# Gate and up of a decoder layer as seven half-block products instead of eight

## The chip, the cores and the metric

The kernel runs on one core of a Trainium2 chip. The time is the device time of one execution in microseconds (us); the median of several executions is compared. A profile is taken of one execution and shows each engine's instructions: TensorE (PE, with its weight loads as PEld), VectorE (DVE), ScalarE (ACT), GpSimd (POOL) and SyncE (SP), which issues most of the DMA transfers.

## The reference

One decoder layer on 512 tokens of width 1024, all in float32. An input projection feeds two groups of mixers, a gated linear recurrence and an attention with three branches; their outputs go through an output projection and are added to x. Then comes the part that is changed:

```
h   = rms_norm(x, ffn_norm_w)
out = x + (silu(h @ w_gate) * (h @ w_up)) @ w_down      # 1024 -> 2816 -> 1024
```

## The kernel before

A float32 value enters TensorE as two parts, a high one (rounded to float32r) and a low one (the remainder). A product of two such values is three matmuls: high by high, high by low, low by high (`mm3`, L98 to L101; each matmul is L96). The parts are made on the chip: ScalarE casts the high one, VectorE subtracts it from the value (`weights`, L130 to L153). Where `weights` is told to use GpSimd (12 pieces of the input projection) VectorE is left out: ScalarE writes the negated value, rounded to float32r, into the low tile (L149), and GpSimd issues a DMA that adds the raw value onto it (L150), which leaves the low part. A weight piece is 512 KB; it is loaded into one of three buffers "raw" by SP (L112), and becomes a pair of tiles "whi" and "wlo" with four buffers each.

The order of the instructions is not that of the code alone. A planner simulates the program with costs of its own and lays each engine's instructions into one fixed queue: of those that it holds ready it takes the one that comes first in the code. So matmuls of the feed-forward part may stand between those of the attention. Each engine then runs its queue in order, and SP its transfers.

The attention goes through the token tiles 3, 2, 1, 0 of 128 tokens. When a tile's attention is done, `out_proj` (L864) multiplies its rows with the output weights (12 matmuls of 512 columns for each half of the width, both halves in bank 0) and adds them to the residual `x_sb` (L871), which stays in the on-chip memory. `norm2` (L873) normalises the tile (squares L878, the root on GpSimd L201, the product L884), transposes it in two blocks of 4 x 128 columns (h2p) and splits each into high and low (L890, L891) in the array `ar`. `ar[:, 1]` holds tokens 256 to 511, `ar[:, 0]` tokens 0 to 255.

Gate and up are made in groups of 256 columns of the hidden width, two units of 128 columns each. `load_group` (L938) loads and splits the group's four pieces. `gate_up` (L946) makes, for each unit, 8 steps over the width times 3 matmuls for gate (bank fg) and as many for up (fu), then silu and the product (L956 to L958), and splits the result into high and low (L959, L107). The first two groups (`SPLIT`, L963 to L967) are made in token halves: tokens 256 to 511 first, while tiles 1 and 0 are still under way, then tokens 0 to 255. The other nine groups take all 512 tokens in one matmul. The down projection (fd, L973 to L1003) then runs over the 22 units twice, for each half of the output width, adds the residual and stores.

Of the kernel before, what the change touches and what calls it, by code (L numbers as in the profile page):

```python
# [20 lines left out]
P = 128  # L21
T = 512
# [27 lines left out]
def hybrid_layer(ctx, tc, x, pos, pack, w_in, gate_a, gate_x, qnw, knw, ck1, ck2, cv1, cv2, w_out, fnw, w_gate, w_up, w_down, out):  # L50
# [5 lines left out]
    wst = ctx.enter_context(tc.tile_pool(name="wst", bufs=4))  # L56
# [11 lines left out]
    SLOTS = {"qk": 16, "yr": 8, "rt": 8, "y": 4, "tr": 6}  # L68
# [13 lines left out]

    def small(shape, s, dt=F32, bufs=None):
        return sml.tile(shape, dt, tag=s, name=nm(s), **({} if bufs is None else {"bufs": bufs}))
# [10 lines left out]
    def mm(o, l, r, start, stop):  # L95
        PE.matmul(o, lhsT=l, rhs=r, start=start, stop=stop)  # L96

    def mm3(o, l, r, start, stop):  # L98
        mm(o, l[0], r[0], start, False)
        mm(o, l[0], r[1], False, False)  # L100
        mm(o, l[1], r[0], False, stop)  # L101
# [15 lines left out]
    def weights_in(src, tag):  # L117

        raw = wst.tile([P, 4, 256], F32, tag="raw", bufs=3, name=nm("raw"))
        load(raw, src)  # L120
        out_ = []
        for u in range(2):
            hi, lo = (b2(n, F32R, tag=tag) for n in ("wxh", "wxl"))
            rv = raw[:, 2 * u : 2 * u + 2].rearrange("p a b -> p (a b)")
            S.copy(hi, rv)
            lo_of(lo, rv, hi)
            out_ += [(hi[:, a * 256 : (a + 1) * 256], lo[:, a * 256 : (a + 1) * 256]) for a in range(2)]
        return out_

    def weights(src, a, b, lo_eng=None, row=None, halves=False):  # L130


        raw = wst.tile([P, 1024], F32, tag="raw", bufs=3, name=nm("raw"))
        rv = raw[:, : a * b].rearrange("p (a b) -> p a b", a=a)
        load(rv, src)
        hi = wst.tile([P, 1024], F32R, tag="whi", name=nm("whi"))
        lo = wst.tile([P, 1024], F32R, tag="wlo", name=nm("wlo"))
        n = a * b
        if row is not None:
# [13 lines left out]
        return [tuple(t[:, : a * b].rearrange("p (a b) -> p a b", a=a)[:, i] for t in (hi, lo)) for i in range(a)]  # L153


    x_sb = per.tile([P, NT, D], F32, name="x_sb")
# [5 lines left out]
    def load_x(t):  # L162
        load(x_sb[:, t], x[t * P : (t + 1) * P])
# [57 lines left out]
    def x_half(hf):  # L221
        for k in range(0, KC, 2):
            pt = rot("xT", (4, 5, 6, 7))
            for c in range(2):
                for t in range(2):
                    tp(pt[:, (2 * c + t) * P : (2 * c + t + 1) * P], x_sb[:, 2 * hf + t, (k + c) * P : (k + c + 1) * P])
# [6 lines left out]
    def x_stats():  # L233
        for t in range(NT):
            jk = b2("jk", tag="qk")
            jk2 = b2("jk", tag="qk")
            ss2 = small([P, 2], "ss2")
            after(S.activation(jk, x_sb[:, t, :512], AF.Square, accum_out=ss2[:, 0:1]), pins["x"])
            after(S.activation(jk2, x_sb[:, t, 512:], AF.Square, accum_out=ss2[:, 1:2]), pins["x"])
# [7 lines left out]
    def proj_cm(c0, banks):  # L247
# [3 lines left out]
        def step(w, k, a0, a1):  # L251
            for m in range(4):
                l = tuple(p[:, m * P : (m + 1) * P] for p in w)
                mm3(wide(acc[m][:, a0:a1], a1 - a0), l, hT(k, a0, a1), k == 0 and a0 == 0, k == KC - 1)
# [21 lines left out]
    for t in range(NT):  # L276
        dg = b2("dg", tag="qk")[:, :P]
# [81 lines left out]
    gwr = wst.tile([P, 8, P], F32, tag="raw", bufs=3, name="gwr")  # L359
# [5 lines left out]
    gwh = [b2("gwh", F32R, tag="qk") for _ in range(2)]  # L365
    gwl = [b2("gwl", F32R, tag="qk") for _ in range(2)]
# [14 lines left out]
    for m in range(4):  # L381
# [6 lines left out]
        h, l = b2("xch", F32R, tag="qk"), b2("xcl", F32R, tag="qk")  # L388
# [61 lines left out]
    va = per.tile([P, NT, 2, 2, HD + 1], F32, tag="va", name="va")  # L450
# [5 lines left out]
    zs = []  # L456
    for m in range(4):
        z = b2("z", tag="qk")
# [4 lines left out]
    for m in range(4):  # L463
        tg = []
        for j in range(2):
            pg = rot("pg", (4, 5, 6, 7))
            mm3(pg, (gwh[j][:, m * P : (m + 1) * P], gwl[j][:, m * P : (m + 1) * P]), (xch[m], xcl[m]), True, True)
            tt = b2("tg", tag="yr")
# [565 lines left out]
```

## Time and profile before

| | |
|---|---|
| median of 3 runs | 677.62 us (676.41 to 678.36) |
| the profiled execution | 674.98 us |
| its span, first to last instruction | 673.3 us |
| PE busy / share of the span | 653.8 us / 97% |
| PEld | 541.8 us / 80% |
| DVE | 340.9 us / 51% |
| ACT | 253.2 us / 38% |
| POOL | 40.7 us / 6% |
| mean granted TensorE clock | 0.995 of full speed |

An instruction is named by its line, its engine and what it writes and reads by the program's names. Times of the trace count from the first instruction. Matmuls overlap one another in the pipeline, so their pace is read from the chain of waits (many in a row) and not from the length of one. A DMA's time to landing counts from its issue.

### The profile page before, as it was taken

The numbers are of one execution on the slowest core, as the hardware profiler recorded it, in microseconds if no ns is written. First come the engines' busy times: TensorE is split into PE (matmuls) and PEld (weight loads), VectorE is DVE, ScalarE is ACT, GpSimd is POOL, SyncE is SP. The second block draws the span as 40 slices with busy tenths as digits, with TensorE's granted clock in tenths as the row PEclk, the third lists the DMA queues.
The fourth block names the chain that finished last, engine by engine and source line by source line (L and its number), as shares of the span: only waits on it lengthen the run. The fifth ranks groups of instructions, "written<-read, shape, count | busy, mean of one in ns | idle before, by whom it ended". The sixth has DMA issues, their size and how long they took to land.

```text
span 673.3 us, 8843 instructions
## 1 busy us (share of the span) xinstructions
PE 653.8 (97%) x3486; PEld 541.8 (80%) x3486; DVE 340.9 (51%) x738; ACT 253.2 (38%) x421; POOL 40.7 (6%) x70
## 2 busy tenths in 40 slices
PE   7999989899999999999899999999999999999998
PEld 6878778667788787898798888888888888888886
DVE  6483999865656475956333334434443442223211
ACT  6657958743343343525123223322332232112110
POOL 2111100211001010110000000000000000000000
PEclk9999999899999999999899999999999999999999
DMA  7589743181110010322122244223422343333201
GB/s 264 129 223 203 165 91 115 49 298 65 63 41 24 1 33 0 95 63 91 35 59 68 64 125 125 64 62 125 126 64 63 123 126 93 94 125 126 94 1 62
DMA packets 46914, 64.61 MB, mean 96 GB/s; under 512 B 4052, under 2 KB 32024, under 8 KB 46872
## 3 DMA queue, kind: packets, MB, share of 16 engines
q1 hardware_dynamic: 45064, 57.71, 27.1%
q0 software_dynamic: 1728, 6.29, 5.0%
q8 instruction: 27, 0.44, 0.3%
q14 instruction: 15, 0.12, 0.1%
q10 hardware_dynamic: 80, 0.03, 0.0%
HBM read 55.64 MB, written 2.10 MB: 86 GB/s over the span
## 4 chain that ended last, share of the span: by engine, by line
PE 75%; DVE 8%; issue 7%; DMA 5%; ACT 4%; POOL 1%; POOLq 0%; SPq 0%; DVEq 0%; ACTq 0%
PE fd L96 18%; PE fg L96 18%; PE fu L96 17%; PE po L96 4%; PE por L96 3%; PE sT L96 3%; DMA raw<-in_w_in_dram 3%; PE pw L96 3%; PE s L96 2%; PE ph L96 2%; DMA wlo<-raw 1%; DMA raw<-in_ck_dram 1%; ACT whi L146 1%; PE oc L96 1%; PE ptm L96 1%
## 5 line engine op out<-in xcount | busy, mean ns | idle before, releaser
L152 DVE TENSOR_TENSOR wlo<-raw,whi 128x1024 fp32r<-128x1024 f32 (+2 forms) x73 | 86.4, 1185 | 118.3 <-ACT whi L146 118.3
L146 ACT CAST whi<-raw 128x1024 fp32r<-128x1024 f32 (+2 forms) x85 | 86.8, 1024 | 151.4 <-PE fd L96 75.4
L96 PE MATMUL fu<-ar,whi 128*128 128x512 f32 (+1 forms) x352 | 102.0, 375 | 0.0
L96 PE MATMUL fg<-ar,whi 128*128 128x512 f32 x288 | 90.5, 395 | 0.0
L96 PEld LDWEIGHTS fu<-ar,whi 128*128 128x128 f32 x352 | 63.8, 188 | 13.1
L96 PE MATMUL fd<-wlo,gh 128*128 128x512 f32 (+1 forms) x189 | 69.3, 367 | 0.0
L96 PE MATMUL fd<-whi,gh 128*128 128x512 f32 (+1 forms) x189 | 69.2, 366 | 0.0
L96 PE MATMUL fd<-whi,gl 128*128 128x512 f32 (+1 forms) x189 | 68.9, 366 | 0.0
L96 PE MATMUL fu<-ar,wlo 128*128 128x512 f32 (+1 forms) x176 | 65.8, 375 | 0.1
L96 PEld LDWEIGHTS fg<-ar,whi 128*128 128x128 f32 x288 | 54.1, 188 | 13.0
L96 PE MATMUL fg<-ar,wlo 128*128 128x512 f32 x144 | 57.0, 396 | 0.0
L96 PE MATMUL ptm<-whi,ar 128*128 128x512 f32 (+1 forms) x192 | 53.5, 360 | 2.1 <-DVE qraw L531 1.9
L958 DVE SCALAR_TENSOR_TENSOR ft<-ft,fu 128x512 f32<-128x512 f32 (+1 forms) x26 | 15.7, 605 | 51.2 <-PE fu L96 51.2
L96 PEld LDWEIGHTS po<-va,pe 128*128 128x128 f32 x320 | 39.6, 192 | 2.2 <-ACT pe L815 0.9
L96 PE MATMUL pcm<-ar,whi 128*128 128x512 f32 (+1 forms) x160 | 41.3, 354 | 0.0
L96 PE MATMUL po<-va,pe 128*128 128x65 f32 x320 | 41.0, 272 | 0.3 <-ACT pe L815 0.2
L96 PEld LDWEIGHTS ptm<-whi,ar 128*128 128x128 f32 x192 | 34.3, 188 | 8.1 <-DVE qraw L531 2.3
L96 PEld LDWEIGHTS fd<-whi,gh 128*128 128x128 f32 x189 | 35.6, 189 | 6.1
L96 PEld LDWEIGHTS fd<-wlo,gh 128*128 128x128 f32 x189 | 35.6, 189 | 5.9
L96 PEld LDWEIGHTS fd<-whi,gl 128*128 128x128 f32 x189 | 35.6, 188 | 5.8
L96 PEld LDWEIGHTS fu<-ar,wlo 128*128 128x128 f32 x176 | 33.0, 188 | 6.9 <-DVE wlo L152 0.3
L957 DVE SCALAR_TENSOR_TENSOR ft<-ft,fg 128x512 f32<-128x512 f32 (+1 forms) x26 | 15.6, 604 | 41.3 <-ACT ft L956 41.3
(316 smaller groups left out, 1097.9 us busy)
## 6 DMA issues: line engine op xcount, KB each, us to landing
raw<-in_w_gate_dram SPq DMA_DIRECT2D x22, 512.0 KB, 3.6
raw<-in_w_up_dram SPq DMA_DIRECT2D x22, 512.0 KB, 3.5
raw<-in_w_down_dram SPq DMA_DIRECT2D x22, 512.0 KB, 3.9
raw<-in_w_in_dram SPq DMA_DIRECT2D x16, 512.0 KB, 4.7
wlo<-raw POOLq DMA_DIRECT2D x12, 512.0 KB, 5.9
raw<-in_w_out_dram SPq DMA_DIRECT2D x8, 512.0 KB, 4.5
x_sb<-in_x_dram SPq DMA_DIRECT2D x4, 512.0 KB, 7.8
raw<-in_ck_dram SPq DMA_DIRECT2D x4, 512.0 KB, 4.6
```

The costliest lines, as they stand in the source:

```text
L96: PE.matmul(o, lhsT=l, rhs=r, start=start, stop=stop)
L146: S.copy(hi[:, c], raw[:, c])
L152: (lo_eng or V).tensor_tensor(out=lo[:, c], in0=raw[:, c], in1=f(hi[:, c]), op=ALU.subtract)
L957: V.scalar_tensor_tensor(out=tt, in0=tt, scalar=1.0, in1=pg[:, :nn], op0=ALU.add, op1=ALU.mult)
L958: V.scalar_tensor_tensor(out=tt, in0=tt, scalar=0.5, in1=pu[:, :nn], op0=ALU.mult, op1=ALU.mult)
```

## The change

Gate and up are written as one product of 2 x 2 blocks. A block of the left side is 128 columns of w_gate (A11, A12) or of w_up (A21, A22) by one half of the width; a block of the right side is one half of the width of h by one half of the tokens (B11, B21: tokens 256 to 511; B12, B22: tokens 0 to 255). Instead of eight products of blocks, seven are made, with sums S1 to S4 of blocks of weights and T1 to T4 of blocks of h (Strassen's identity in Winograd's form): A11 B11, A12 B21, S4 B22, A22 T4, S1 T1, S2 T2, S3 T3. Each is 4 pieces x 3 matmuls of 256 columns. Several are added up in one PSUM bank, and ScalarE copies or VectorE adds the running sum out between two of them.

- Sums S are made by VectorE from raw weights (`sums`), and then split; A11 and A12 (`set_gate`) and A22 are split with the DMA that adds (`by_dma`), S1 to S4 by VectorE. `pin` fixes the order of these instructions on each engine.
- Weight loads change from 256 columns by 4 rows to 128 columns by 8 rows per partition (pieces of 512 bytes), still 512 KB each. "whi" and "wlo" become one set of 12 buffers "w"; "raw" keeps 3.
- `norm2` makes two blocks of each of the tiles 3 and 2, and five of each of the tiles 1 and 0.
- Three units (`EARLY`) make A11 B11 and A12 B21 ahead, the rest of all units in one loop, in which the last two products of a unit stand among the first of the next.
- The results of gate and up stay whole until the loop is over; they are split then, into the places of the blocks of h.
- x after the attention goes to a tensor in device memory (`x2`) and is loaded again for the last addition. The scratch for GpSimd's descriptors is 2048.
- In the input projection the matmuls over 512 tokens are made as two of 256.

The core of the diff:

```diff
-    SLOTS = {"qk": 16, "yr": 8, "rt": 8, "y": 4, "tr": 6}
+    SLOTS = {"rt": 8, "y": 4, "tr": 6, "gx": 6}
...
+    def raw_tile(s):
+        return wst.tile([P, 1024], F32, tag="raw", name=nm(s), bufs=3)
+
+    def w_tile(s, dt=F32R):
+        return wst.tile([P, 1024], dt, tag="w", name=nm(s))
...
-                step(ws[a], 2 * kk + a, 0, T)
+                step(ws[a], 2 * kk + a, 0, 256)
+                step(ws[a], 2 * kk + a, 256, T)
...
+        load(x2_dram[i * P : (i + 1) * P], x_sb[i])
...
+        if not late:
+            xn_of[i] = xn
+            for hf in range(2):
+                normed(hf)
+                put(xn[hf], ("11", "21")[hf])
+            return
+        xo = xn_of[i + 2]
+        normed(1)
+        normed(0)
...
+        V.tensor_tensor(out=t3, in0=xn[1], in1=xn[0], op=ALU.subtract)
+        V.tensor_tensor(out=xn[0], in0=xo[0], in1=xn[0], op=ALU.subtract)
+        V.scalar_tensor_tensor(out=t2, in0=xn[1], scalar=-1.0, in1=xn[0], op0=ALU.mult, op1=ALU.subtract)
+        V.scalar_tensor_tensor(out=xo[1], in0=t2, scalar=-1.0, in1=xo[1], op0=ALU.mult, op1=ALU.subtract)
+        for src, n in ((t2, "T2"), (xn[0], "T1"), (t3, "T3"), (xo[1], "T4"), (xn[1], "22")):
+            put(src, n)
...
+    def split(src, hi, lo, by_dma=False):
+        pin("S", S.copy(hi, src))
+        if by_dma:
+            pin("S", S.activation(lo, src, AF.Copy, scale=-1.0))
+            pin("G", G.dma_start(out=lo, in_=src.bitcast(F32R), accum_op=ALU.add))
+        else:
+            pin("V", V.tensor_tensor(out=lo, in0=src, in1=f(hi), op=ALU.subtract))
...
+    def sums(u, r1):
+        r2, sa, sb = raw_tile("r2"), x_tile("sa"), x_tile("sb")
+        w_cols(w_up, u, r2)
+        a11, a12, a21, a22 = r1[:, :512], r1[:, 512:], r2[:, :512], r2[:, 512:]
+        pin("V", V.tensor_tensor(out=sa[:, :512], in0=a21, in1=a22, op=ALU.add))
+        pin("V", V.tensor_tensor(out=sb[:, :512], in0=sa[:, :512], in1=a11, op=ALU.add))
+        pin("V", V.tensor_tensor(out=sb[:, 512:], in0=sb[:, :512], in1=a12, op=ALU.add))
+        pin("V", V.tensor_tensor(out=sa[:, 512:], in0=a11, in1=a21, op=ALU.add))
+        return r2, sa, sb
+
+    def set_sums(u, r2, sa, sb):
+        o = split(sb, w_tile("h"), w_tile("l"))
+        A[u]["S2"], A[u]["S4"] = o[:4], o[4:]
+        o = split(sa, w_tile("h"), w_tile("l"))
+        A[u]["S1"], A[u]["S3"] = o[:4], o[4:]
+        if u < 12:
+            p22 = [b2("p22", F32R, tag="rt") for _ in range(2)]
+        else:
+            p22 = [cst.tile([P, 544], F32R, tag="misc", name=nm("p22"), bufs=3)[:, :512] for _ in range(2)]
+        A[u]["22"] = split(r2[:, 512:], *p22, True)
+
+    def product(o, u, a, b, start):
+        for c in range(4):
+            mm3(o, A[u][a][c], tuple(z[:, c] for z in B[b]), start and c == 0, c == 3, skip_group_check=not start)
...
+    for u in range(NU + 1):
+        if u < NU:
+            g_tile(u)
+            r1 = gate_weights(u)
+            ss = sums(u, r1)
+            if u >= EARLY:
+                set_gate(u, r1)
+            set_sums(u, *ss)
...
+                product(acc_b[u], u, "11", "11", True)
+                S.copy(s1, acc_b[u])
+        if u > 0:
+            product(acc_b[u - 1], u - 1, "22", "T4", False)
+        if EARLY <= u < NU:
+            acc_a[u] = half("fa", 4 + u % 4)
+            product(acc_a[u], u, "12", "21", True)
+            V.tensor_tensor(out=gs[u][:, 256:], in0=acc_a[u], in1=s1, op=ALU.add)
+        if u > 0:
+            product(acc_c[u - 1], u - 1, "S4", "22", False)
+            finish_unit(u - 1)
+        if u < NU:
+            product(acc_b[u], u, "S2", "T2", u < EARLY)
...
+                S.copy(v2, acc_b[u])
+            acc_c[u] = half("fc", 2 * (u % 2) + 1)
+            product(acc_c[u], u, "S1", "T1", True)
+            product(acc_b[u], u, "S3", "T3", False)
...
+                S.copy(v3, acc_b[u])
+            V.tensor_tensor(out=v3, in0=acc_c[u], in1=v3, op=ALU.add)
...
-    nc = _bacc.Bacc("TRN2", target_bir_lowering=False, num_devices=1)
+    nc = _bacc.Bacc("TRN2", target_bir_lowering=False, num_devices=1, dynamic_dma_scratch_size=2048)
```

`finish_unit` adds the bank of S1 T1 and S4 B22 to the copy of A11 B11 and S2 T2 (256 columns), takes the tanh of 512 columns on ScalarE and makes one product of 512 and two of 256 on VectorE.

## Rows read from the trace of the kernel before

**Rows 1.** The page: busy us (share) x instructions; the chain by line.
```profile
PE 653.8 (97%) x3486; PEld 541.8 (80%) x3486; DVE 340.9 (51%) x738; ACT 253.2 (38%) x421; POOL 40.7 (6%) x70
...
PE fd L96 18%; PE fg L96 18%; PE fu L96 17%; PE po L96 4%; PE por L96 3%; PE sT L96 3%; DMA raw<-in_w_in_dram 3%; PE pw L96 3%; PE s L96 2%; PE ph L96 2%; DMA wlo<-raw 1%; DMA raw<-in_ck_dram 1%; ACT whi L146 1%; PE oc L96 1%; PE ptm L96 1%
```

**Rows 2.** The chain in time: start us, us, what, count.
```profile
342.04 2.72 PE fg L96 x24
...
347.48 5.59 PE fg L96 x24
...
543.47 5.60 PE fu L96 x24
549.07 121.08 PE fd L96 x594
```

**Rows 3.** Timeline at the last norm: start us, us, engine, line, count, [idle before].
```profile
303.52 0.69 DVE L107 TENSOR_TENSOR yl<-yTp,yh 128x512 fp32r<-128x512 f32 x1 [1.25 <-ACT yh L854]
...
316.90 0.75 DVE L871 SCALAR_TENSOR_TENSOR x_sb<-pw,ra,x_sb 128x512 f32<-128x512 f32 x1
...
321.45 1.42 DVE L884 SCALAR_TENSOR_TENSOR xn<-x_sb,r,fbc 128x512 f32<-128x512 f32 x2 [0.44 <-POOL r L201]
323.57 0.69 DVE L891 TENSOR_TENSOR ar<-h2p,ar 128x512 fp32r<-128x512 f32 x1 [0.70 <-ACT ar L890]
...
322.26 0.65 PE L104 MATMUL h2p<-ident,xn 128*128 128x128 f32 x4 [3.52 <-DVE xn L884]
```

**Rows 4.** Windows: stretch, length, busy us PE PEld DVE ACT POOL, clock, DMA share.
```profile
306.00:314.00 8.00, 7.87 (x52) 7.00 (x51) 5.12 (x7) 3.70 (x6) 0.00 (x0) 1.00 0.27 79
314.00:322.00 8.00, 4.74 (x33) 4.20 (x31) 5.72 (x11) 4.12 (x7) 0.83 (x1) 1.00 0.55 176
322.00:327.00 5.00, 4.07 (x21) 3.83 (x22) 2.24 (x4) 1.17 (x2) 0.00 (x0) 0.66 0.03 10
```

**Rows 5.** DMA issues: queue, count, KB each, median us to landing.
```profile
raw<-in_w_in_dram SPq DMA_DIRECT2D x16, 512.0 KB, 4.7
```

**Rows 6.** Packets, MB, share of 16 engines: whole span, 350:549, 549:673 us.
```profile
q0 software_dynamic: 1728, 6.29, 5.0%
...
q1 hardware_dynamic: 17627, 18.77, 30.7%
...
q1 hardware_dynamic: 5927, 11.02, 27.4%
```

**Rows 7.** Input projection: chain, GpSimd's timeline, landings of its DMAs.
```profile
26.39 4.78 DMA wlo<-raw
...
31.24 4.55 DMA raw<-in_w_in_dram
...
38.17 1.05 POOL L150 DMA_DIRECT2D wlo<-raw  x1 [8.88 <-ACT wlo L149]
...
L150 POOL DMA_DIRECT2D wlo<-raw x12: 859/862/1074, 26.4 to 85.4; - x12
...
DMA to landing us min/median/max: 4.5/5.9/8.4
```

**Rows 8.** Groups by form from 200 us on: count, busy us, mean ns.
```profile
L146 ACT CAST whi<-raw 128x1024 fp32r<-128x1024 f32 x60 | 63.3, 1055 | 139.5 <-PE fd L96 75.4 <-PE fg L96 27.0 <-PE fu L96 16.8
...
L956 ACT ACTIVATE ft<-fg 128x512 f32<-128x512 f32 x18 | 10.7, 593 | 38.3 <-PE fg L96 38.3
...
L743 ACT COPY pcs<-pc 128x256 f32<-128x256 f32 x2 | 0.7, 353 | 0.0
...
L152 DVE TENSOR_TENSOR wlo<-raw,whi 128x1024 fp32r<-128x1024 f32 x60 | 73.5, 1224 | 114.8 <-ACT whi L146 114.8
...
L107 DVE TENSOR_TENSOR gl<-ft,gh 128x512 fp32r<-128x512 f32 x17 | 11.7, 689 | 6.2 <-ACT gh L959 6.2
...
L958 DVE SCALAR_TENSOR_TENSOR ft<-ft,fu 128x256 f32<-128x256 f32 x8 | 3.3, 419 | 7.1 <-PE fu L96 7.1
```

More of the change, by code (lines that the diff above doesn't have):

```diff
@@ L93, in after, with mm, mm3 @@
         return ins
[L95 to L101, printed above, removed]
+    def mm(o, l, r, start, stop, **kw):
+        PE.matmul(o, lhsT=l, rhs=r, start=start, stop=stop, **kw)
+    def mm3(o, l, r, start, stop, **kw):
+        mm(o, l[0], r[0], start, False, **kw)
+        mm(o, l[0], r[1], False, False, **kw)
+        mm(o, l[1], r[0], False, stop, **kw)
     def tp(o, i, n=P):
@@ L356, in hybrid_layer @@
     V.tensor_scalar(rwn, par[:, R_RW : R_RW + 4], -0.5, None, ALU.mult)
-    gwr = wst.tile([P, 8, P], F32, tag="raw", bufs=3, name="gwr")
+    gwr = raw_tile("gwr").rearrange("p (a b) -> p a b", b=P)
     G.memset(gwr, 0.0)
@@ L447, in dup @@
         return ap.unsqueeze(2).to_broadcast([ap.shape[0], nh, 2, HD])
[L450 removed]
+    va = cst.tile([P, NT, 2, 2, HD + 1], F32, tag="va", name="va")
     G.memset(va[:, :, :, :, HD : HD + 1], 1.0)
@@ new lines, in hybrid_layer, with pin @@
+    chain = {}
+    def pin(k, i):
+        if k in chain:
+            after(i, chain[k])
+        chain[k] = i
+    def split(src, hi, lo, by_dma=False):
[5 more added lines that the diff above has]
+            pin("V", V.tensor_tensor(out=lo, in0=src, in1=f(hi), op=ALU.subtract))
+        return [(hi[:, c * P : (c + 1) * P], lo[:, c * P : (c + 1) * P]) for c in range(src.shape[1] // P)]
@@ new lines, in half, with finish_unit @@
+    def half(s, n):
+        return bank(s, n)[:, :256]
+    acc_a, acc_b, acc_c = {}, {}, {}
+    def finish_unit(u):
+        gate, up, s1, v2, ft = hold[u]
+        if u < EARLY:
+            V.tensor_tensor(out=up[:, 256:], in0=acc_b[u], in1=s1, op=ALU.add)
+        V.tensor_tensor(out=gate[:, :256], in0=acc_c[u], in1=v2, op=ALU.add)
+        S.activation(ft, gate, AF.Tanh, scale=0.5)
+        V.scalar_tensor_tensor(out=gate, in0=ft, scalar=1.0, in1=gate, op0=ALU.add, op1=ALU.mult)
+        if u < EARLY:
+            V.scalar_tensor_tensor(out=gs[u], in0=gate, scalar=-0.5, in1=up, op0=ALU.mult, op1=ALU.mult)
+        else:
+            V.scalar_tensor_tensor(out=gs[u][:, :256], in0=gate[:, :256], scalar=-0.5, in1=up[:, :256], op0=ALU.mult, op1=ALU.mult)
+            V.scalar_tensor_tensor(out=gs[u][:, 256:], in0=gate[:, 256:], scalar=-0.5, in1=acc_b[u], op0=ALU.mult, op1=ALU.mult)
@@ new lines, in hybrid_layer, with g_tile @@
+    gtags = [t for t in ("gx", "y", "rt") for _ in range(SLOTS[t])]
+    def g_tile(u):
+        if u < 4:
+            if u % 2 == 0:
+                gs.extend(b4("g"))
+        else:
+            gs.append(b2("g", tag=gtags.pop(0)))
+    ahead = {}
+    for u in range(EARLY):
+        mk = w_tile if u < 2 else (lambda s: qkp.tile([P, 1024], F32R, tag="qk", name=nm(s), bufs=8))
+        set_gate(u, gate_weights(u), mk)
+        acc_a[u] = half("fa", 4 + u % 4)
+        product(acc_a[u], u, "11", "11", True)
+        xe = cst.tile([P, 544], F32, tag="misc", name=nm("xe"), bufs=3)[:, :512]
+        S.copy(xe[:, :256], acc_a[u])
+        product(acc_a[u], u, "12", "21", False)
+        S.copy(xe[:, 256:], acc_a[u])
+        ahead[u] = xe
@@ L972, in hybrid_layer @@
     NK = DF // P
     TAIL = 4
+    gl_tags = ["tr"] * 2 + ["qk"] * 4 + ["gx"] * 6 + ["y"] * 4 + ["rt"] * 6
+    gh_at = [z.rearrange("p c q -> p (c q)")[:, o : o + 512] for n in ("11", "21", "T2", "T1", "T3", "T4") for z in B[n] for o in (0, 512)]
+    gh = []
+    for k in range(NK):
+        h = gh_at[k]
+        S.copy(h, gs[k])
+        if gl_tags[k] == "qk":
+            if k % 2 == 0:
+                pair = b4("gl", F32R)
+            l = pair[k % 2]
+        else:
+            l = b2("gl", F32R, tag=gl_tags[k])
+        lo_of(l, gs[k], h)
+        gh.append((h, l))
```

211 lines of the change are left out of this document (109 added, 102 removed).

## The prediction

> **What bounds the kernel now.** I read the busy shares of the page first, then the chain of waits in order of time, then windows around the one place where the chain leaves TensorE, then the DMA views. TensorE is busy for 97% of the span, and 35% of the chain is gate and up (fg, fu), 18% the down projection [rows 1]. In order of time [rows 2] each row of 24 matmuls from 347.48 to 549.07 us takes 5.60 us and starts where the last one ends: TensorE never waits there, so only fewer or shorter matmuls can shorten this stage, unless something else becomes late. The same rows price the two shapes: 5.60/24 = 0.2333 us for a matmul of 512 columns, 2.72/24 = 0.1133 us for one of 256. A half-width matmul, with a weight load of its own, costs slightly less than half of a full one. The change lives on that. [...]
>
> **Matmuls.** A unit is 128 columns of gate and of up; there are 22. Before, a unit is 2 x 8 x 3 = 48 full matmuls: 18 units x 48 x 0.2333 = 201.6 us, which is 347.48 to 549.07, and the four split units are 4 x 96 x 0.1133 = 43.5 us. After, a unit is 7 products x 4 pieces x 3 = 84 half matmuls, 9.52 us: 22 x 84 x 0.1133 = 209.4 us. So 35.7 us of TensorE time go. That is the ceiling. The input projection's 144 full matmuls become 288 halves, 33.6 to 32.6 us; that stage waits for transfers [rows 7], so I take nothing, between -1 and +1.
>
> **The start.** Some of the 35.7 us is given back here. Before, 192 half matmuls (21.8 us) on tokens 256 to 511 can run beside the end of the attention; after, only 3 x 24 = 72 (8.2 us). All others need sums over both token halves, so they wait for the norm of the last tile. I rebuild its time from the instructions there [rows 3]: the last attention rows are split at 303.52 + 0.69 = 304.2; 12 output matmuls follow (2.8 us), their addition (0.75), 12 more in the same bank, and the second addition. Before, the second addition ends at 317.65, because fu matmuls stand in TensorE's queue between the two groups; without them I get 304.3 + 2.8 + 1.0 + 2.9 + 0.9 = 311.9. From that addition to the normed rows (316.90 + 0.75 to 321.45) it is 3.8 us, so 315.7; two normalisations and three differences on VectorE, five instructions of about 0.69 (the 512 form of L107) [rows 8], give 319.1; transposing, casting and subtracting T2 takes another 2.2 (322.26 to 324.26 is 2.0 before), so 321.3. I take 322. If the queue keeps its old order it is 317.65 + 3.8 + 3.4 + 2.2 = 327; if planning finds more room, 319. Each of the two late tiles now makes five blocks and four sums: 3 more pairs of cast and subtraction and 4 sums per tile, some 9.4 us more on VectorE. It was busy for 5.12 + 5.72 + 2.24 of the 21 us from 306 to 327 [rows 4], partly with gate and up's own subtractions, which go. So these fit, but the weight sums of units 0 to 2 (4 x 0.6 + 2 x 1.15 = 4.7 us each) compete with them: I take 2 us of delay, from 0 to 8. TensorE will have stood still before it; 5 us at 0.66 is 1.7 us lost, and I take 1.7 again (0 to 4).
>
> **The loop, engine by engine.** ScalarE per unit: four casts or negations of 1024 (1.055 each), two of 512 (0.6), a tanh of 512 (0.6), three copies of 256 out of a bank (0.353 each) [rows 8]: 7.1 us. VectorE: two subtractions of 1024 (1.22), four sums and one product of 512 (0.69), five of 256 (0.42): 8.0 us. Both below 9.52, both above two thirds of it, and each now hands something to TensorE several times per unit: the three copies out of the banks must be done before the next product may add to that bank. The shortest distance is one product, 12 x 0.1133 = 1.36 us, against 0.35 plus at most one cast of 1.05 in front: just enough, so tenths at worst.
>
> **The raw ring.** This is the doubtful part. Each unit loads two raw tiles, as before, into three buffers. But now a raw tile whose low part comes by accumulating DMA is held until that DMA has read it, where VectorE freed it before. The input projection shows such a cycle: the DMA is issued at 26.39, lands after 4.78, the next load into the buffer lands 4.55 after 31.24, and that piece's DMA starts at 38.17: 11.8 us a turn [rows 7]. With the medians (load 4.7 [rows 5], 2.0 for two ScalarE instructions, 0.3 to the issue, landing 5.9 [rows 7]) a gate tile holds its buffer for 12.9 us. An up tile: 4.7, three sums (2.0), four ScalarE instructions (two of 1.0, two of 0.6: 3.2), 0.3, and a landing of half the size, between 2.9 and 5.9, say 4.4: 14.6. Together 27.5 us over three buffers is 9.2 us a unit; with 1 us in each tile's turn for other work of ScalarE and VectorE it is 9.8. At the shortest landings (4.5, and half of it) and without that work it is 8.0, so TensorE bounds; at the longest (8.4, and three quarters of it) 10.6. I take 9.8 us a unit, 0.3 over TensorE's own pace.
>
> **The transfers.** One core's 16 DMA engines carry it all. The accumulating DMA moved 6.29 MB in 5.0% of 16 engines over 673.3 us, 33.7 us [rows 6]: 0.79 MB a unit is 4.2 us. Loads: 18.77 MB in 30.7% of 199 us, 307 GB/s with pieces of 1024 bytes [rows 6]; 1.05 MB is 3.4 us. The new loads have pieces of 512 bytes, which no row shows. By packets, the loads of 350 to 549 us took 61.1 x 16/17627 = 55.5 ns for 1065 bytes, those of 549 to 673 us 34.0 x 16/5927 = 91.7 ns for 1859 bytes; a line through both gives 30 ns for 512 bytes, 3.9 us a unit, so 8.1 of 9.52 us. From above: if a half packet costs what a whole one does, 6.8 + 4.2 = 11.0 us a unit, and the DMA engines bind. I take the line, since the two measured sizes already show cost falling with size. [...]
>
> **The rest.** The 22 splits of the products into high and low parts move behind the loop: 0.6 each on ScalarE and VectorE, against 24 x 0.23 = 5.6 us of TensorE per two of them, and their first tiles come free during the last unit: nothing, at most 3 us at the start of down if they queue behind the last unit's work. The residual goes out to memory and back (2 x 2 MB) at times with idle DMA engines: nothing, at most a load behind it on SP's queue, 4 us once. The smaller scratch for GpSimd's descriptors costs nothing unless the issue (0.86 us, POOL 1.05 at 38.17) begins to wait for landings, which would be the ring at 10.6. The down projection keeps its matmuls: 121.08 us.
>
> **The sum.** 322 + 3 units x 60 x 0.1133 (20.4) + 1.7 + 2 = 346.1; 19 units x 9.8 = 186.2 give 532.3, where down starts; before it is 549.07. So 16.8 us less: 674.98 (the profiled run) becomes 658.2. The median of the runs shown is 2.6 us above the profiled run, so 661.
>
> **Rivals.** (a) Everything hides and TensorE alone binds: 319 + 20.4 + 1.7 + 19 x 9.52 = 522, 27 us less, 651 as a median. For it: ScalarE and VectorE have at least a sixth of each unit free, and short landings give a ring of 8.0. (b) The DMA engines or the ring bind: 11.0 us a unit, 346.1 + 209 = 555, 6 us later than now, 684. It decides from (549.07 - 346.1)/19 = 10.7 us a unit on. For it: the longest landing, and a DMA share that goes from 0.31 to 0.85 while the landings were read at far lower shares. Against: at 11 us the share falls again, and the ring of the input projection turned with landings below 6 us. (c) A late start: the old queue order and VectorE as the bound of units 0 to 2: 327 + 20.4 + 1.7 + 8 = 357, + 186.2 = 543, 672. (d) From unit 13 on the low part of A22 goes to one of three "misc" tiles, which the product of the unit before must have released, and ScalarE's fixed order puts the next gate split behind it: two products (2.7), 0.3, one instruction of 0.6 and two of 1.0, 0.3, a landing of 4.8 to 5.9: 10.7 to 11.8 a unit, so 8 units x 1.5 = 12 more, 673, unless the planner lets that product run ahead of the next unit's first. Or the change doesn't do what it says: the planner lays ScalarE's copies out of the banks behind splits that wait for a load, and TensorE waits at each product; 1.2 us a unit brings it to (b).
>
> **Chances.** Forecast (652 to 669) 0.47, (a) 0.18, (b) 0.18, (c) 0.08, (d) 0.09. A measurement here can tell about 0.3%, 2 us, from nothing. Faster is the forecast, (a), (c), (d) less their spill, and the mildest edge of (b): 0.78; the same 0.05; slower 0.17. Range 648 to 684, which takes in (a) and most of (b); the likeliest case's own is 652 to 669.
>
> **What would show it.** Matmuls of 256 columns at 0.113 us and 84 to a unit; units 9.6 to 10.0 us apart from the fourth on; the first T2 product at 319 to 325 us with a low granted clock; SP's loads waiting for the accumulating DMA. Wrong if units are over 10.7 us apart, if the DMA share in the loop is at 0.95, or if half matmuls come at more than 0.12 us.

## The result, and the profile after

The changed kernel takes 733.3 us as a median of four runs (730.7, 732.7, 733.9 and 748.5; the last was a disturbed run and is not in the ratio), the kernel before 677.8: 1.0815 times as long, 95% interval 1.0784 to 1.0846. The forecast was 661, range 648 to 684. The profiled execution took 730.69 us, its span 729.0. The page of the changed kernel, as [rows 1]: busy times, and the chain by engine ("issue" is time for which the profile names no wait; in the loop it stands behind GpSimd's issues of the transfers).

```profile
PE 657.4 (90%) x4254; PEld 578.1 (79%) x4254; DVE 430.0 (59%) x913; ACT 336.8 (46%) x564; POOL 74.5 (10%) x114
...
PE 51%; issue 26%; ACT 7%; DVE 7%; DMA 7%; POOL 2%; POOLq 0%; SPq 0%; ACTq 0%; DVEq 0%
```

TensorE is busy for about as long as before (657.4 us against 653.8), though the count of matmuls takes 35.7 us away: in the windows shown below a half matmul takes 83.31/661 = 0.126 and 88.66/677 = 0.131 us of busy time, not 0.1133. And it is busy for 90% of the span, not 97%: it waits now. Where, the times of a few products and of one addition tell, read by tile.

| | before | after |
|---|---|---|
| first matmul of the recurrence's output (por) | 154.5 | 172.9 |
| end of the attention's last addition | 317.65 | 322.93 |
| first product with T2 (fb) | - | 338.0 |
| last product of gate and up | 549.1 | 609.3 |
| span | 673.3 | 729.0 |

So 18 us are late in the front (all that comes ahead of the output products) already, attention gives 13 of them back (by the trace 184 half matmuls of gate and up stood among its own before, and 48 now), 15 pass until the sums are there, and gate and up then take 271 us. Its pace is best read from ScalarE's tanh, one to a unit (timeline: start us, us, engine, line, ..., [idle before]); these are units 3, 11, 12 and 20:

```profile
384.63 0.62 ACT L1043 ACTIVATE xa<-g 128x512 f32<-128x512 f32 x1
...
478.10 0.64 ACT L1043 ACTIVATE xa<-g 128x512 f32<-128x512 f32 x1 [4.46 <-DVE g L1042]
...
487.31 0.62 ACT L1043 ACTIVATE xa<-g 128x512 f32<-128x512 f32 x1
...
594.75 0.63 ACT L1043 ACTIVATE xa<-g 128x512 f32<-128x512 f32 x1
```

That is 93.47/8 = 11.68 us a unit from 3 to 11 and 107.44/8 = 13.43 from 12 to 20; before, a unit was 11.2. The windows of these stretches (length, busy us of PE, PEld, DVE, ACT, POOL; clock, DMA share, GB/s):

```profile
384.00:478.00 94.00, 83.31 (x661) 80.36 (x661) 57.84 (x95) 50.08 (x77) 12.82 (x15) 0.98 0.63 149
487.00:595.00 108.00, 88.66 (x677) 85.82 (x676) 57.81 (x94) 57.89 (x93) 13.38 (x16) 0.95 0.68 160
```

No engine is full, and the DMA engines are not either: what sets the unit is a turn of waits, as the experiments below bear out. One turn of the middle units, from the timeline of all engines:

```profile
430.24 1.05 ACT L989 CAST h<-r 128x1024 fp32r<-128x1024 f32 x1 [2.75 <-PE fc L104]
431.20 1.05 ACT L991 ACTIVATE l<-r 128x1024 fp32r<-128x1024 f32 x1
...
432.60 0.85 POOL L992 DMA_DIRECT2D l<-r  x1 [3.90 <-ACT l L991]
...
437.91 0.39 PE L104 MATMUL fa<-ar,l 128*128 128x256 f32 x1 [0.89 <-DMA l<-r]
...
442.12 1.05 ACT L989 CAST h<-r 128x1024 fp32r<-128x1024 f32 x1 [2.81 <-PE fc L104]
```

ScalarE's cast of a gate pair waits for a product (fc, the S4 B22 of an earlier unit) that frees its place in the ring of 12, the set of buffers that the weight tiles take turns in; 2.0 us later the negated copy is there, 0.35 later GpSimd issues the accumulating transfer, 5.3 us after that TensorE goes on with the low part; and the product that frees the next place stands behind it in TensorE's queue. 430.24 to 442.12 is 11.9 us, the unit. From unit 12 on the same turn is longer by one link: ScalarE's negated copy of A22 waits for a product of the unit before, and the gate pair's cast stands behind it.

```profile
509.79 0.63 ACT L991 ACTIVATE p<-r 128x512 fp32r<-128x512 f32 x1 [0.99 <-PE fb L104]
510.33 1.04 ACT L989 CAST h<-r 128x1024 fp32r<-128x1024 f32 x1
510.79 0.85 POOL L992 DMA_DIRECT2D p<-r  x1 [11.91 <-ACT p L991]
511.27 1.05 ACT L991 ACTIVATE l<-r 128x1024 fp32r<-128x1024 f32 x1
...
512.68 0.85 POOL L992 DMA_DIRECT2D l<-r  x1 [1.05 <-ACT l L991]
...
518.09 0.39 PE L104 MATMUL fa<-ar,l 128*128 128x256 f32 x1 [2.08 <-DMA l<-r]
```

### The profile page after: what moved, and what is told of

It is laid out like the page before. It is cut to its first block, busy times and chain, and to the rows that moved or that the text cites. A ratio compares the mean times of both kernels' runs of the same rounds, so it can differ in the third digit from the quotient of the medians.

```text
span 729.0 us, 10847 instructions
## 1 busy us (share of the span) xinstructions
PE 657.4 (90%) x4254; PEld 578.1 (79%) x4254; DVE 430.0 (59%) x913; ACT 336.8 (46%) x564; POOL 74.5 (10%) x114
## 4 chain that ended last, share of the span: by engine, by line
PE 51%; issue 26%; ACT 7%; DVE 7%; DMA 7%; POOL 2%; POOLq 0%; SPq 0%; ACTq 0%; DVEq 0%
PE fd L104 17%; PE pcm L104 6%; PE ptm L104 5%; PE po L104 4%; DMA r<-in_w_up_dram 3%; PE pw L104 3%; PE por L104 3%; PE sT L104 3%; PE s L104 2%; PE ph L104 2%; POOL l L992 1%; DMA raw<-in_w_in_dram 1%; ACT whi L145 1%; DMA raw<-in_cv_dram 1%; PE fa L104 1%
## 5 line engine op out<-in xcount | busy, mean ns | idle before, releaser
L145 ACT CAST whi<-raw 128x1024 fp32r<-128x1024 f32 (+2 forms) x47 | 46.7, 996 | 94.7 <-PE fd L104 65.9
L151 DVE TENSOR_TENSOR wlo<-raw,whi 128x1024 fp32r<-128x1024 f32 (+2 forms) x35 | 39.8, 1138 | 59.7 <-ACT whi L145 59.7
L104 PE MATMUL fb<-T,h 128*128 128x256 f32 x352 | 66.2, 286 | 6.1 <-ACT xa L1105 5.0
L104 PEld LDWEIGHTS fb<-T,h 128*128 128x128 f32 x352 | 55.0, 191 | 7.9 <-ACT xa L1105 6.3
L1011 DVE TENSOR_TENSOR sa<-r 128x512 f32<-128x512 f32 x22 | 15.2, 692 | 62.1 <-DMA r<-in_w_up_dram 62.0
L104 PE MATMUL fb<-T,l 128*128 128x256 f32 x176 | 50.0, 284 | 0.0
L104 PE MATMUL pcm<-ar,whi 128*128 128x256 f32 x256 | 46.5, 287 | 0.0
L104 PE MATMUL fa<-ar,h 128*128 128x256 f32 x200 | 41.2, 300 | 0.5 <-ACT xe L1068 0.5
L104 PE MATMUL fd<-whi,T 128*128 128x512 f32 (+1 forms) x108 | 40.1, 371 | 0.0
L104 PE MATMUL fd<-wlo,T 128*128 128x512 f32 (+1 forms) x108 | 40.1, 371 | 0.0
L104 PEld LDWEIGHTS pcm<-ar,whi 128*128 128x128 f32 x256 | 39.7, 193 | 0.2 <-ACT whi L145 0.2
```

The source lines that it names most:

```text
L104: PE.matmul(o, lhsT=l, rhs=r, start=start, stop=stop, **kw)
L145: S.copy(hi[:, c], raw[:, c])
L151: (lo_eng or V).tensor_tensor(out=lo[:, c], in0=raw[:, c], in1=f(hi[:, c]), op=ALU.subtract)
L1011: pin("V", V.tensor_tensor(out=sa[:, :512], in0=a21, in1=a22, op=ALU.add))
```

## The experiments

A pace is read as above, from unit 3 to 11 and from 12 to 20. The kernel before, run beside these, took 675.5 to 677.8 us as medians, single runs up to 679.6. What is given without a range is one run, and the change stands with its profiled one; its next two lie 2 and 3 us higher, so a difference of 3 us between single runs tells nothing by itself.

| kernel | us | units 3 to 11 | 12 to 20 | first por |
|---|---|---|---|---|
| the change | 730.7 | 11.68 | 13.43 | 172.9 |
| both low parts by VectorE (e1_no_accum) | 691.6 | 10.21 | 10.75 | 174.5 |
| no low part added at all (e6_no_add) | 688.7 | 9.82 | 10.76 | 172.1 |
| gate's by transfer alone (e18_gate_dma) | 697.8 | 11.44 | 10.63 | 171.2 |
| A22's by transfer alone (e20_a22_dma) | 706.3 | 10.86 | 11.03 | 173.0 |
| fourth raw buffer (e5_raw4) | 727.6 | 11.60 | 13.97 | 168.1 |
| A22 in "rt" until unit 17 (e2_misc) | 725.3 | 11.68 | 12.23 | 171.9 |
| rings of 4 and 8 (e3_tags) | 739.3 | 13.72 | 14.21 | 159.1 |

**The transfers.** In the first the accumulating transfer and the negated copy go, in the second the transfer alone (the low parts then stay the negated values).

```
-        o = split(r1, mk("h"), mk("l"), True)
+        o = split(r1, mk("h"), mk("l"))
-        A[u]["22"] = split(r2[:, 512:], *p22, True)
+        A[u]["22"] = split(r2[:, 512:], *p22)
```

> The changed kernel with every low part of the gate/up loop made by VectorE's subtraction (no accumulating transfer, no negated copy on ScalarE). Theory 1, the accumulating transfer sets the unit (it holds the raw buffers that the loads wait for, and its landing of 3.5 to 5.3 us stands between ScalarE's cast and the next unit's first product): units 3 to 12 fall from about 11.1 to 9.5 to 10.0 us, the three first units lose part of their 41 us, units 13 to 21 fall from 12.9 to about 11; in all 705 to 715 us against 730.7. Rival, the ring of 12 weight tiles (ScalarE's casts wait for products three units back) sets it: nothing is gained there, VectorE gets about 1.6 us more a unit (62 us busy of 100 before), 727 to 737 us.

```
-            pin("G", G.dma_start(out=lo, in_=src.bitcast(F32R), accum_op=ALU.add))
```

> The changed kernel with the accumulating transfers of the gate/up loop left out: the low parts are the negated values alone (the addition of the raw values is left out), ScalarE's two passes stay as they are. It takes the transfer away without giving VectorE anything. If the transfer's landing and its hold on the raw buffers set the unit: 700 to 715 us, units 3 to 12 at 9.5 to 10 us. If the ring of weight tiles does: 726 to 732 us. If the loads' bandwidth does (share of the DMA engines 0.67 in units 3 to 12, of which the accumulating transfers are about a quarter): in between, 715 to 725 us, with the loads' landings falling below 3.8 us.

39 and 42 us go, more than either theory had. The tanh of units 3, 11, 12 and 20 of the first, and its window over units 3 to 11:

```profile
380.06 0.64 ACT L1043 ACTIVATE xa<-g 128x512 f32<-128x512 f32 x1
...
461.75 0.63 ACT L1043 ACTIVATE xa<-g 128x512 f32<-128x512 f32 x1
...
470.86 0.63 ACT L1043 ACTIVATE xa<-g 128x512 f32<-128x512 f32 x1 [3.31 <-DVE g L1042]
...
556.85 0.64 ACT L1043 ACTIVATE xa<-g 128x512 f32<-128x512 f32 x1
```

```profile
380.00:461.00 81.00, 79.04 (x661) 78.16 (x659) 70.70 (x111) 39.61 (x64) 0.00 (x0) 1.00 0.38 110
```

TensorE is busy for 79.0 of 81 us: it bounds there, with VectorE at 70.7 close behind. That VectorE was spared work (1.6 us a unit) had been paid for with TensorE's time. Gate and up loads landed after 3.8 and 3.7 us in this stretch, and after 4.3 and 3.8 in the change (372 to 472 us), so bandwidth has at most a small part in it. The 3 us between the two kernels are too few for single runs to tell, but units 3 to 11 are 0.4 us shorter in the second, which spares VectorE the subtractions and keeps ScalarE's negated copies.

Do they cost by holding the raw buffers, as the prediction feared, or by their landing?

```
-        return wst.tile([P, 1024], F32, tag="raw", name=nm(s), bufs=3)
+        return wst.tile([P, 1024], F32, tag="raw", name=nm(s), bufs=4)
-    fbc = cst.tile([P, D], F32, name="fbc")
+    fbc = raw_tile("fbc")
```

> The changed kernel with a fourth raw buffer (the norm's weight row, 4 KB, is kept in one until the last norm), all accumulating transfers left as they are. If they cost by holding raw buffers: the waits of VectorE for the up load (20.5 us in units 3 to 12, 27.2 in 13 to 21) go, units 3 to 11 fall from 11.7 to about 10.2 us, 705 to 715 us. If they cost by their landing between ScalarE's cast and the product: units stay at 11.2 to 11.7 and 724 to 731 us.

VectorE's wait for the up load from 384 to 478 us, in the waits of the change and of this kernel (us in total, times, longest):

```profile
DVE sa L1011 <- DMA r<-in_w_up_dram: 19.9, 8, 3.8
```
```profile
DVE sa L1011 <- DMA r<-in_w_up_dram: 1.2, 1, 1.2
```

The wait goes, and the unit stays at 11.6 us. So the buffers were not the bound, though that wait stood high in the table: VectorE, busy for 57.84 of these 94 us in the change, had time for it. Next, one transfer at a time (each one of the two edits of the first experiment):

> The changed kernel with A22's low part by VectorE and only the gate pair's by the accumulating transfer. If each transfer costs by holding its raw buffer, half the 39 us go or more, since the up buffer is then free early: 705 to 715 us. If the gate transfer's landing ahead of the unit's first product is what counts: 722 to 731 us. If only the sum of bytes counts (256 of 768 KB gone): about 718 us.

> The changed kernel with the gate pair's low part by VectorE and only A22's by accumulating transfer. If the two transfers cost apart from each other, the gate's in units 3 to 11 by its landing ahead of the product, A22's from unit 12 on in the misc slots: units 3 to 11 at 10.2 to 10.6 us, units 12 to 21 at 12.5 to 13.5, 712 to 722 us. If either transfer alone is enough to slow units 3 to 11: 11.2 us and more there, and 722 to 731 us.

Both totals are missed: each lies below every case that was named. The gate's transfer alone leaves units 3 to 11 at 11.44, as its landing ahead of the product says, but it costs only 6 us in all; A22's alone costs 15, with units of 8 and 13.6 us in turn from 3 to 11, and 6 of the 15 in the last unit (21.2 us, against 15.2 with neither); both together 39. From unit 12 to 20 each alone costs little (10.6 and 11.0, 10.75 with neither) and the two together make 13.4: the turn shown above needs both, A22's place and the gate's landing behind it.

**A22's places.** `if u < 12:` becomes `if u < 18:`.

> The changed kernel with A22's two tiles in the tag rt until unit 17 rather than until unit 11, so that the three misc slots serve units 18 to 21 alone. If the misc slots make the later units slow (ScalarE's cast of A22 waits 20.6 us for earlier products in units 13 to 21): units 12 to 17 stay at about 11.1 us rather than 12.9 and one unit of 16 to 19 us is gone or moves to unit 18; 714 to 722 us. If another wait takes its place (the up load, the accumulating transfer): less than 4 us, 727 to 732 us.

5 us of the 9 to 17 expected; units 12 to 17 come 12.5 us apart (491.33 to 553.74) where 11.1 was expected. So the three misc slots are part of it. ScalarE's negated copy of A22 waits for a product for 4.6 us in total over these units, where it waited 18.7 in the change; the gate's cast waits for fc instead (11.5), and why the unit is still longer than 11.7 is open. With the transfers gone, five slots instead of three (the norm's weight row gives up its 4 KB):

> The first experiment's kernel (no accumulating transfer in the gate/up loop), with five misc slots rather than three: the norm's weight row, 4 KB before, takes two of them until the last norm. If the three misc slots set the units from 12 on (10.75 us apart without the transfer, against 10.2 of units 3 to 11; ScalarE's copy out of the bank waits 27.3 us there): units 12 to 20 at 10.1 to 10.3, 4 to 6 us less, 685.5 to 688 us against 691.6. If it is another wait: 690 to 693 us.

689.0 us: units 12 to 20 at 10.41 rather than 10.75, 2.7 us, about half of what was expected.

**The front.** Is it the halved input projection? The kernel before with this part alone:

```
-                step(ws[a], 2 * kk + a, 0, T)
+                step(ws[a], 2 * kk + a, 0, 256)
+                step(ws[a], 2 * kk + a, 256, T)
```

> The kernel before with one part of the change alone: the later pieces of the input projection in halves of 256 tokens, the halves of one token half ahead of those of the other. Theory: this part costs nothing, 674 to 680 us with the kernel before at 676 to 678, and the output products still start at 154 to 155 us. Rival: the halved pieces make the front late (16 to 18 us after the whole change), 685 to 695 us.

677.05 us beside 677.2 (675.75 to 678.61): it costs nothing that shows. Then the rings:

```
-        return wst.tile([P, 1024], dt, tag="w", name=nm(s))
+        return wst.tile([P, 1024], dt, tag="w", name=nm(s), bufs=8)
+    def t_tile(s, dt=F32R):
+        return wst.tile([P, 1024], dt, tag="t", name=nm(s), bufs=4)
     (tg, yr and the gate pairs of all units but the third: t_tile)
```

> The changed kernel with the recurrence's tiles (tg, yr) in a ring of their own (4 tiles of 1024) and the weights in a ring of 8, as much memory as the ring of 12; in the loop the gate pairs use that ring of 4, so that each pair waits for the pair of two units before only. Theory on the front (the tg tiles stand in the same ring as the weights' splits, so that the q projection's weights wait for them): the rnn output products start at about 155 rather than 173.1 us, which is 16 to 18 us less, if attention does not give it back. In the loop the theory of the ring of 12 expects 0.5 to 1.5 us less a unit, the theory of the accumulating transfer no change. In all 712 to 716 us by the front alone, 695 to 710 with both. Rival for the front (the halved pieces of the input projection or the planner's order made it late): 728 to 733 us.

The low halves of the output product's matmuls in the change, with the split alone and with the two rings (by tile: count, ns, first and last start):

```profile
L104 PE MATMUL por<-wlo,yr x32: 387/389/396, 173.3 to 215.4; 128*128 128x512 f32 x32
```
```profile
L96 PE MATMUL por<-wlo,yrh x32: 387/389/398, 156.6 to 194.8; 128*128 128x512 f32 x32
```
```profile
L104 PE MATMUL por<-wlo,yr x32: 387/389/501, 159.4 to 200.1; 128*128 128x512 f32 x32
```

The front comes 14 us earlier, of the 16 to 18 expected. But the loop pays some 20, and the 739.3 us lie above every case: each gate pair now waits for the pair two units back, the landing is in that turn too, and units 3 to 11 come 6 and 19 to 24 us apart in turn. In the change's own timeline the place can be seen: ahead of q's first cast (that of the ninth weight piece) ScalarE stands idle for 4.5 us and then runs seven tanh and four more steps of the recurrence, whose tiles come ahead of q's weights in the ring.

```profile
53.12 1.28 ACT L479 ACT_TABLE_LOAD   x1
58.92 1.37 ACT L479 ACTIVATE tg<-pg,hb 128x512 f32<-128x512 f32 x2 [4.52 <-PE pg L104]
...
65.86 1.06 ACT L145 CAST whi<-raw 128x1024 fp32r<-128x1024 f32 x1
```

Before, that cast ran at 46.86. Two other ways to the same end, on the first experiment's kernel: the q projection written ahead of the tg products (two blocks of code exchanged),

> The first experiment's kernel with the q projection written ahead of the recurrence's first products, so that the weights of q take their places in the ring ahead of the four tg tiles; the ring stays one of 12. If the order of places in the ring made the front late: q's matmuls start at 56 to 58 rather than 66.9 us, the output products at 160 to 165 rather than 174.5, and 8 to 14 us are gone: 678 to 684 us against 691.6. If the ring's size does it (fewer places while tg and yr are held): less than 4 us.

and the tg and yr tiles in other places, the ring of 12 kept (with five slots and the pad below):

> VectorE's low parts, five misc slots, the pad of 64 bytes, the ring of 12 for the weights, and the recurrence's tg and yr tiles outside that ring (in the tag of the norm's rows, and the fourth pair in two misc slots). If their places in the ring made the front late: the output products start at 155 to 160 us, the units stay at 10.0 to 10.2 us, 669 to 673 us, which is faster than before the change. Rival: the front got late by something that the split rings changed beside (fewer weight tiles in flight): 682 to 686 us.

The first is a clear miss: 710 us, q's matmuls do start at 58.2, but the recurrence's first products move from 57.9 to 80.6 and the output products to 186.5. The second gives 680.4 us (677.6 to 683.2; ratio to before 1.0048, 1.0026 to 1.0069), output products at 167.8: 5 to 6 us, not 14. From 60 to 80 us TensorE is busy for 14.1 us there, at a granted clock of 0.83 and a DMA share of 0.93:

```profile
60.00:80.00 20.00, 14.13 (x49) 10.85 (x48) 9.01 (x17) 15.62 (x22) 3.79 (x7) 0.83 0.93 216
```

So the places of tg and yr in the ring of 12 are part of the front's cause. The raw buffers are in it too: the fourth one (e5_raw4) brought the output products from 172.9 to 168.1. The rest stays open. The same kernel with the three early gate pairs by transfer:

> The same with the low parts of the three early gate pairs by accumulating transfer, where VectorE is busy for all of 330 to 340 us: 1.1 us of VectorE each go from the end of the attention. If VectorE sets the start of the first sums' products: 1 to 3 us less than without. If the raw buffers held by these transfers delay the loads of units 0 and 1: 1 to 5 us more.

679.2 us, no difference that one run can tell.

**The matmul's pace.** After the change half matmuls come every 0.1183 us (the median distance of the starts of gate and up's is 0.118), before every 0.1133 [rows 2]. The halves of the input projection show it as well, where the loop plays no part: the median distance of their starts is 0.113 us in the kernel before and 0.117 in the change, and in the change's chain 140 of them in a row take 16.57 us, 0.1184 each. On the first experiment's kernel: the pad ahead of the weights' ring (an unused tile that shifts what lies behind it) taken out, or doubled.

```
-    pad.tile([P, 8], F32, name="pad_k")
+    pad.tile([P, 16], F32, name="pad_k")
```

> The first experiment's kernel without the pad of 32 bytes ahead of the weights' ring, so that weights, raw tiles and all that lies behind them start 32 bytes lower, at the same remainder by 64 bytes as the activations, as they did before the change. Theory, the matmul's pace depends on where its operands lie: half matmuls come every 0.117 us after the change (median of 0.113 before, the input projection's halves too, which are the same instruction) and fall back to 0.113: some 2400 half matmuls times 0.004 is 8 to 10 us less, 682 to 684 us against 691.6. Rival, the pace comes from the shape of the loop (weights and banks changing more often): no change in the pace, 690 to 693 us. A third possibility: the transfers get slower by the shift (loads land later than 3.7 us), 693 to 700 us.

> The first experiment's kernel with a pad of 64 bytes rather than 32 ahead of the weights' ring: weights at 32, activations at 96 of each 128 bytes, the two remainders that they had before the change (now 0 and 96; with 96 and 96 half matmuls came every 0.120 us and full ones every 0.227). If the two remainders alone set the pace: half matmuls every 0.113 us rather than 0.117, and 5 to 9 us less, 683 to 687 us against 691.6. If not: 690 to 693 us.

691.7 and 686.9 us against 691.6. The chain in time of the three kernels (pad of 32, 0 and 64 bytes; start us, us, what):

```profile
395.91 1.42 PE fc L104 x12
```
```profile
396.55 1.44 PE fc L103 x12
```
```profile
395.37 1.36 PE fc L104 x12
```

Twelve half matmuls take 1.42, 1.44 and 1.36 us, the commonest times in the chain of each kernel from 395 to 430 us, so 0.1183, 0.120 and 0.1133 (in the third, twelve take 1.41 us from 416 us on): the first shift was a miss in the wrong direction, the second is the pace of before. Units 3 to 11 fall from 10.21 to 10.03 us.

**Together.**

> The three edits of this group together on the first experiment's kernel: five misc slots, no pad, q first. If each theory holds and the gains add (5 + 9 + 11 us): 664 to 670 us, faster than before the change by 1 to 2%. If the front's gain is lost again in attention, or if VectorE (70 of 80 us busy in the loop) becomes the bound as the matmuls get faster: 672 to 680 us.

> No accumulating transfer in the gate/up loop, five misc slots, and the rings of the third experiment: 4 tiles for tg, yr and the loop's gate pairs, 8 for the other weights. Theory: the rings gave 14 us in the front and cost 20 in the loop only because a transfer's landing stood in the shorter turns; without the transfer a turn of two units is long enough. Then the front is 12 to 14 us earlier and the units stay at 10.2 to 10.5 us: 674 to 678 us against 689.0 for the same without the rings. Rival: two units are too short a turn whatever makes the low part, units at 11 us and more, and 690 to 705 us.

> The same as the kernel with five misc slots, VectorE's low parts and the split rings, with the pad of 64 bytes as well. If rings and remainders both do what their theories say: 667 to 672 us, 1% faster than before the change. If the rings cost in the loop: 685 to 700 us. If the remainders do nothing: 674 to 678 us, the same as before the change.

The first holds the failed order of q: 705.9 us. The second 678.5, units at 10.5 to 10.6, output products at 159.4. The third, with the pad of 64 bytes, is the best: 676.05 us (674.3 to 676.7 in ten runs), ratio to the kernel before 0.9978, interval 0.9966 to 0.999. That is the range that was named for a pad that does nothing, and the pad doesn't shorten the units here: 10.63 and 10.53 us, without it 10.64 and 10.49, some 7.6 and 13.5 in turn. So with the split rings the pace is not what sets the unit. Last, the pairs spread over both rings (each third unit's gate and sb pair and the next unit's sa pair in the ring of 4):

> The kernel with split rings, VectorE's low parts, five misc slots and the pad of 64 bytes (676.05 us), with the pairs spread over the two rings: gate and sb pairs of each third unit and the sa pair of the unit after stand in the ring of 4, all others in the ring of 8, so that no pair waits for its own kind of two units before. If that wait cost the 0.5 us a unit: units 3 to 20 at 10.0 to 10.2 us rather than 10.5 and an uneven 7.6 and 13.4, 666 to 670 us, faster than before the change by 1.0 to 1.6%. If VectorE (near 90% busy) sets the unit: 673 to 677 us.

676.6 us (673.2 to 678.6), ratio 0.9983 (0.9966 to 1.0). Units 3 to 11 come 10.08 us apart, as expected, but 12 to 20 at 10.64, and the total does not move. Its window over units 3 to 18:

```profile
366.00:530.00 164.00, 156.91 (x1333) 154.31 (x1333) 141.89 (x225) 82.15 (x130) 0.00 (x0) 1.00 0.39 115
```

TensorE 96%, VectorE 87%. A half matmul takes 156.91/1333 = 0.1177 us of busy time here, 9.9 us for the 84 of a unit, so some of the distance from 9.52 is TensorE's own busy time. That the rest comes from the hand-overs between the two engines is a reading of these shares; no run tests it.

## Why the prediction was wrong

The sum went wrong at two steps, by 16 and by 61 us; the end gave 4.5 of them back, and 72.5 is the distance of the profiled run from its 658.2.

**The start, 322 forecast, 338.0 measured.** It was worked out from the old times of the attention, as if nothing ahead of it moved. But the output products start 18.4 us late. "That stage waits for transfers, so I take nothing" holds for the halved matmuls (e14_only_split); what was not costed is that tg and yr moved into the weights' ring. With rings of their own 14 of the 18 us go, with tg and yr elsewhere and the ring kept 5 to 6, so the move is a part of the cause and the rest is open. The step read the edit's instructions, and this edit has none. Attention then took 13.1 us less from the output products to the last addition, where my rebuild had 5.7; and from that addition to T2 15.1 us passed, not 10.1. 18.4 - 7.4 + 5.0 is the 16. The weight sums of a unit stood at 4 x 0.6 + 2 x 1.15 = 4.7 us; at the 0.69 and 1.22 of [rows 8] they are 5.2. The 1.7 us for the clock were the row from 322 to 327 us of [rows 4], 5 us at 0.66. Between 322 and 338 us of the change VectorE is busy for 13.41 of 16 us and the granted clock is 0.79 (1.00 from 338 to 343 us):

```profile
322.00:338.00 16.00, 10.98 (x66) 9.25 (x64) 13.41 (x22) 11.94 (x22) 2.29 (x3) 0.79 0.58 145
```

**The unit, 9.8 us forecast, 11.7 and 13.4 measured.** From T2 to the last product I had 210.3 us, and it is 271.3. Little of the difference lies ahead of the fourth unit: from the first product with T2 to the third tanh (338.0 to 370.1 us) TensorE ran 257 half matmuls, 77 more than three units have. The step that failed is the price of a unit, taken from the turn of the raw ring. That turn is not the one that binds: with a fourth raw buffer the unit stays at 11.6 us (e5_raw4). The sign that I had named for it came all the same, SP's loads waiting for the accumulating transfers (51.2 and 48.6 us over units 3 to 11, and 51.1 and 47.4 with the fourth buffer). The raw turn counts a transfer's landing against the buffer that it reads; the tile that it writes has a turn too: freed by a product, cast, negated, issued, landed, used by a product. That turn I never wrote down for the ring of 12, although its terms stand in [rows 7] and [rows 8]: 2.0 + 0.35 + 5.3 and some 4 us of products is 11.9. Without the transfers the unit is 10.2 (e1_no_accum). Rival (b) gave 11.0 and 684 for another reason; its condition, over 10.7 us a unit, came true. The landings of [rows 7] were not read at far lower shares than 0.85: from 26 to 86 us of the kernel before the DMA share is 0.83.

**Rival (d)** named the second turn with its place and links, and gave it 0.09 and 12 us. The place was right (units 12 to 21, ScalarE's copy of A22 behind a product, the gate's cast behind that), the size too small: 13.4 us a unit, against my 10.7 to 11.8, since, as the timeline has it, the turn holds the rest of the first one too; with either transfer alone it is 10.6 and 11.0.

**Matmuls.** 84 halves to a unit are there; the pace is 0.1183 rather than 0.1133. The 0.005 by 84 by 22 are 9.2 us of TensorE, a quarter of the ceiling of 35.7, and where TensorE bounds, moving one pad took 4.7 us off (e12_shift96). Taking over a duration from [rows 2] assumed that it does not depend on where the tiles lie.

**What held.** The transfers' cost: q1 moved 17680 packets in 30.9% of 16 engines from 372 to 472 us, 28 ns a packet of 512 bytes, where the line gave 30, and the accumulating 6.82 MB took 35.8%, 5.25 us a MB, where [rows 6] gives 5.35.

```profile
q0 software_dynamic: 2438, 6.82, 35.8%
q1 hardware_dynamic: 17680, 8.91, 30.9%
```

By the 28 ns the loads are 3.6 us a unit, where the line gave 3.9. The input projection, the down projection's start and the residual's trip to memory cost nothing that shows; from the last product of gate and up to the end it is 4.5 us less than before, since 31 of the down projection's 594 matmuls have run by then.

**Where the saving went in the best version** (e15_best). Its transfers are gone, its front is early, most of its half matmuls have the median length of e12_shift96's, 276 ns (281 in e1_no_accum), and it is level with the kernel before. From its first product with T2 (324.3 us) to the end of its last product of gate and up (556.1) pass 231.8 us, where 1776 half matmuls at 0.1133 take 201.2: some 31 us are lost in the units, 20 of them as 19 units of 10.6 rather than 9.52. Another 13.6 went as the prediction said: before, 21.8 us of half matmuls fitted beside the end of the attention, after it 8.2. Together that is more than the 35.7; the end gives some 7 back, as 35 matmuls of the down projection have run by then.

## What to carry to other kernels

When a copy moves from an engine to a transfer, write down the turn of every tile that it reads and every tile that it writes, from freed to freed, landing included; here the longest of them, 11.9 us, was the unit of 11.7, and the table of waits did not say which it was. When tiles change their ring, look at what stands ahead of them there, even where the edit adds no instruction. Arithmetic that is saved on a full engine is worth its time only if the others can hand it work at the new pace: here, with VectorE at 87% of the loop, a unit fell from 11.2 to 10.6 us where 9.52 was to be had, and no run tells what holds it there.

## What the runs showed of the hardware

**A half matmul's pace differed with the place of the weights.** With a pad of 64, 32 and 0 bytes ahead of the weights' ring, and no other edit between the three kernels, half matmuls come every 0.1133, 0.1183 and 0.120 us in the chain from 395 to 410 us (e12_shift96, e1_no_accum, e8_shift32). The mean granted clock of the three executions is 0.975, 0.977 and 0.978, lowest where the pace is fastest. The difference does not hold throughout: from 416 us on twelve take 1.41 us in the first kernel as well, 0.1175 each. The pad moves the weights, and all that lies behind them, against the blocks of h. By the layout that stands with e12_shift96 the weights then start 32, 0 and 96 bytes behind a multiple of 128 and the activations at 96; the traces show no addresses. Why the pace changes is not settled by these runs.

**An accumulating transfer within the core's memory landed later than the gate and up loads of its size.** In the change the medians are 5.3 us for 512 KB and 3.5 for 256 KB, and 4.4 and 4.0 for the loads of 512 KB:

```profile
r<-in_w_gate_dram SPq DMA_DIRECT2D x25, 512.0 KB, 4.4
l<-r POOLq DMA_DIRECT2D x22, 512.0 KB, 5.3
r<-in_w_up_dram SPq DMA_DIRECT2D x22, 512.0 KB, 4.0
...
p<-r POOLq DMA_DIRECT2D x22, 256.0 KB, 3.5
```

The second 256 KB are 1.8 us of the 5.3; from 372 to 472 us, where the medians are 5.2 and 3.8, they are 1.4. Single landings of 512 KB lie between 4.4 and 6.7 us, at a DMA share of 0.63 to 0.68 in the loop. Whether that spread comes from what else is in flight, and whether accumulating has a part of its own, is not shown.
